# Two transformer blocks in one kernel: weight transfers in program order, and places for weights apart from places for working tiles

## The chip, the cores and the metric

The kernel runs on 1 core of one Trainium2 chip. The time is that of one execution on the device, in microseconds (us), and the number for a kernel is the median of its runs.

## The reference

The input is one sequence of 256 tokens of 1024 numbers. A first block of two layers and a second block of one follow one another:

```python
for l in range(2):                                  # first block
    h = h + hybrid_mixer(rmsnorm(h, norm_mix[l]), ...)       # dilated + window attention, gated
    h = h + expert_choice_ffn(rmsnorm(h, norm_ffn[l]), ...)  # 16 experts, 32 tokens each
x = rmsnorm(h, norm_final) + sincos                 # second block
s_f, s_b = context_states(hc @ w_in[:, 512:2048], lbs)       # from 256 context tokens
x = x + gt1 * token_mixer(modulate(rms_norm(x), sh1, sc1) @ w_in, ..., s_f, s_b)  # hgrn2 + hyena
x = x + gt2 * hier_moe(modulate(rms_norm(x), sh2, sc2), ...) # 4 groups x 8 experts, top 2
y = rms_norm(x, final_norm_g)
```

An expert of the first block computes silu(a) * u with a, u = its 32 tokens times 1024 x 1024 matrices, and multiplies by a third. The second block's experts are 1024 x 512. The modulation (sh, sc, gt) is a product of a 1024 vector with ada_w. All weights are 32-bit floats; the chip reads 745.74 MB of HBM in an execution.

## The kernel before

Weights stream through SBUF in chunks of 1 MB, [128 partitions x 2048 numbers], each fetched by `K.chunk(src)` (L51): it takes a tile named w with the tag W and issues one transfer on SyncE's queue (SP). The pool gives the tag W PLACES = 21 places of 8 KB per partition. The large working tiles (those named in WHOLE: x, hTa, hTb, V, G, hn, ob and so on) take their places out of the same 21. Small tags (P, PT, wh, wl, oa) have two to four places of 2 KB. The Tile scheduler decides in which order the instructions of an engine stand, SP's transfers among them; a transfer is issued when the place it writes is free, and all later ones on SP's queue stand behind it.

The stages, by the profile's time:
- Mixer 0 and mixer 1 (57 to 300, 637 to 1014): the projections w_in, w_a, w_b, w_o in blocks. Each chunk is split on ScalarE and VectorE into wh (L95) and wl (L96), and TensorE multiplies three times (L115 to L117). While it does so, the 24 chunks of ada are multiplied by the conditioning (L588) and attention goes on.
- Experts of layers 0 and 1 (310 to 637, 1022 to 1489): 128 chunks of w_eg (gate and up; eight a expert, L765) and 64 of w_ed (down, L816), used unsplit. In layer 0, chunks wk of the next layer's projection are computed among w_ed. In layer 1, preparation of the second block (long filter, context states) is woven into the experts. 19 chunks of w_eg are asked for ahead of the loop (PLACES - 2).
- Token mixer (1516 to 1800): chunks w2z, w2q, w2v, w2h, w2g, w2ga, w2gb, w2a, w2b, w2o, split as above. Ahead of it, the residual h is normed (hn, L178), transposed by TensorE (L187) and modulated; `gb` (a 256 KB tile of the tag P, L592) holds the bias of the modulation.
- Experts of the second block (1817 to 2291): per four experts 16 chunks of w2eg (L1427) and 8 of w2ed (L1468). 17 are asked for ahead of it. The last chunk of w2ed does not take a place of W: four quarters of it take three places of wh and one of wl (`quarters`, L62).

The stretches between these are the routers and norms. Small loads (masks, biases, constants; L45, L614, L1010) stand on the same queue.

Of the kernel before, what the change touches and what calls it, by code (L numbers as in the profile page):

```python
# [9 lines left out]
F = mybir.dt.float32  # L10
FR = mybir.dt.float32r
# [21 lines left out]
class Core:  # L33
    def __init__(self, ctx, tc, A):
# [19 lines left out]
    def next_chunk(self, src):  # L54
        return self.pre.pop(0) if self.pre else self.chunk(src)

    def quarters(self, src, tags):

        ts = []
        for i, tag in enumerate(tags):  # L60
            t = self.sb.tile([128, 512], F, name="w4", tag=tag, bufs=SMALL[tag])
            self.nc.sync.dma_start(out=t, in_=src[:, i * 512:(i + 1) * 512])  # L62
            ts.append(t)
        return Quarters(ts)
# [224 lines left out]
PLACES = 21  # L289
# [25 lines left out]
def mixer(K, h, l, ada, first=None, ahead=None):  # L315
# [225 lines left out]
    for c in range(2):  # L541
# [3 lines left out]

        K.row_blocks([K.chunk(A["w_o"][l, 2 * c + i]) for i in range(2)], mT, add, ("sc", "mm")[c])
# [33 lines left out]
def ada_gate(K, g):  # L580
# [11 lines left out]
    nc.sync.dma_start(out=gb, in_=K.A["gtb"][g])  # L592
# [18 lines left out]
def first_loads(K):  # L611
    nc, A = K.nc, K.A
    K.negd = K.t([128, 1280], "negd", tag="cA")
    nc.sync.dma_start(out=K.negd, in_=A["negd"])  # L614
# [3 lines left out]
    nc.sync.dma_start(out=K.wr, in_=A["wr"])  # L618
# [55 lines left out]
def experts(K, h, l, mix, ada, prep, ahead=None):  # L674
# [75 lines left out]
    ws = [K.chunk(A["w_eg"][l, i // KD, i % KD]) for i in range(PLACES - 2)]  # L750
# [105 lines left out]
def context(K):  # L856
# [16 lines left out]
    nc.sync.dma_start(out=cx, in_=A["ctx"])  # L873
# [55 lines left out]
def long_filter(K):  # L929
# [4 lines left out]
    for t, n in ((w1, "hw1"), (w2, "hw2"), (zT, "hz")):  # L934
        nc.sync.dma_start(out=t, in_=A[n])
# [36 lines left out]
    nc.sync.dma_start(out=dft, in_=A["dftf"])  # L972
# [11 lines left out]
def token_mixer(K, h):  # L984
# [279 lines left out]
    K.wr = K.t([128, KD, 64], "wr2", tag="wr")  # L1264
    nc.sync.dma_start(out=K.wr, in_=A["wr2"])
    for c in range(2):
# [6 lines left out]
        K.row_blocks([K.chunk(A["w2o"][c, i]) for i in range(2)], mT, add, ("sc", "mm")[c])  # L1273
# [3 lines left out]
def moe(K, h, mix):  # L1277
# [416 lines left out]
```

## Time and profile before

| | us |
|---|---|
| median of 3 runs | 2315.32 (2307.85 to 2316.28) |
| profiled execution | 2309.24 |
| its span in the profile | 2307.5 |
| TensorE busy | 1843.7 (80%) |
| VectorE, ScalarE, GpSimd busy | 780.5, 584.2, 215.9 |

The DMA engines moved 748.84 MB, a mean of 325 GB/s. A share of 80% for TensorE is a mean over stages: it is over 90% in the mixers and about 70% in the experts.

### The profile page before, as it was taken

To read this page: it belongs to the slowest core of one execution; us is meant where nothing else is said; L and a number is where in the kernel's file an instruction comes from. 1 tells how busy PE (TensorE), PEld (TensorE's weight loads), DVE (VectorE), ACT (ScalarE), POOL (GpSimd) and SP (SyncE) were. 2 spreads that over 40 slices of the span, in tenths; PEclk is the share of its full clock that TensorE was granted. 3 is DMA by queue.
4 is the path that set the end of the run, shared out by engine and by line. 5 is a ranking of instruction groups with operands and counts; after the bars stand their busy time and mean duration, and the time that the engine had idled before them with its cause. 6 is when DMAs were issued, how large, how long until landed. Compare 5 with 4: busy or idle time off the path is not lost. (4 is left out here: it accounts for less than half of the span.)

```text
span 2307.5 us, 30259 instructions
## 1 busy us (share of the span) xinstructions
PE 1843.7 (80%) x12172; PEld 1041.9 (45%) x12172; DVE 780.5 (34%) x1823; ACT 584.2 (25%) x1181; POOL 215.9 (9%) x179
## 2 busy tenths in 40 slices
PE   8999896666699989988678667589999877676665
PEld 7877741110277776742234123268787412121211
DVE  4765530000045687632112011237546311111112
ACT  4555410000032354530126000055235200000000
POOL 2101300000011111300000000034033000000000
PEclk9999997777799988998889788889999999999988
DMA  8335679999999920879999999882114899999996
GB/s 348 111 128 219 246 315 420 420 420 420 419 419 418 409 105 1 349 300 402 420 419 419 419 420 419 331 330 94 72 73 169 329 420 419 420 419 420 419 420 262
DMA packets 108442, 748.84 MB, mean 325 GB/s; under 512 B 14119, under 2 KB 14536, under 8 KB 18696
## 3 DMA queue, kind: packets, MB, share of 16 engines
q1 hardware_dynamic: 107752, 745.79, 79.4%
q8 instruction: 98, 1.61, 0.3%
q10 hardware_dynamic: 544, 1.05, 0.1%
q14 instruction: 48, 0.39, 0.0%
HBM read 745.74 MB, written 1.05 MB: 324 GB/s over the span
## 5 line engine op out<-in xcount | busy, mean ns | idle before, releaser
L765 PE MATMUL mm<-w,xT 128*32 128x512 f32 x2048 | 317.6, 722 | 106.4 <-DMA w<-in_w_eg 106.1
L95 ACT ACTIVATE wh<-w 128x512 fp32r<-128x512 f32 x384 | 234.8, 628 | 306.7 <-PE mm L116 214.8
L115 PE MATMUL mm<-hTa,wh 128*128 128x256 f32 x960 | 283.6, 297 | 14.6 <-ACT wh L95 10.7
L117 PE MATMUL mm<-hTa,wl 128*128 128x256 f32 x960 | 277.0, 293 | 7.8 <-DVE wl L96 6.8
L116 PE MATMUL mm<-hTb,wh 128*128 128x256 f32 x960 | 275.1, 288 | 1.6 <-DVE hTb L107 1.6
L96 DVE TENSOR_TENSOR wl<-w,wh 128x512 fp32r<-128x512 f32 x286 | 212.6, 757 | 113.0 <-ACT wh L95 109.9
L1427 PE MATMUL mm<-w,xT 128*32 128x512 f32 x1024 | 179.2, 625 | 71.7 <-DMA w<-in_w2eg 71.3
L816 PE MATMUL acc<-w,hid 128*32 128x256 f32 x2048 | 176.5, 445 | 63.1 <-DMA w<-in_w_ed 63.1
L96 POOL TENSOR_TENSOR wl<-w,wh 128x512 fp32r<-128x512 f32 x98 | 127.9, 1305 | 921.4 <-ACT wh L95 827.8
L115 PEld LDWEIGHTS mm<-hTa,wh 128*128 128x128 f32 x960 | 185.2, 193 | 36.6 <-ACT wh L95 17.9
L765 PEld LDWEIGHTS mm<-w,xT 128*32 128x32 f32 x2048 | 51.2, 118 | 312.7 <-DMA w<-in_w_eg 250.6
L117 PEld LDWEIGHTS mm<-hTa,wl 128*128 128x128 f32 x960 | 183.4, 193 | 19.4 <-DVE wl L96 9.6
L116 PEld LDWEIGHTS mm<-hTb,wh 128*128 128x128 f32 x960 | 185.5, 193 | 5.3 <-issue 2.8
L816 PEld LDWEIGHTS acc<-w,hid 128*32 128x32 f32 x2048 | 79.9, 127 | 144.7 <-DMA w<-in_w_ed 83.0
L1468 PE MATMUL acc<-w,work 128*32 128x512 f32 x512 | 104.9, 677 | 35.5 <-DMA w<-in_w2ed 32.7
L1427 PEld LDWEIGHTS mm<-w,xT 128*32 128x32 f32 x1024 | 34.7, 111 | 194.2 <-DMA w<-in_w2eg 144.7
L172 POOL TENSOR_TENSOR rs<-rs,mhalf 128x2 f32<-128x2 f32 x9 | 6.7, 748 | 1013.3 <-DVE rs L171 1013.3
L781 DVE TENSOR_TENSOR hid<-tp,sg 128x256 f32<-128x256 f32 x32 | 13.6, 425 | 218.1 <-ACT sg L780 218.1
L107 DVE SCALAR_TENSOR_TENSOR yd<-acc,gw,yd 128x256 fp32r<-128x256 f32 x32 | 15.4, 483 | 173.4 <-ACT yd L106 173.4
L85 DVE COPY gs<-mm 128x512 f32<-128x512 f32 x16 | 11.1, 692 | 176.2 <-PE mm L765 176.2
L1468 PEld LDWEIGHTS acc<-w,work 128*32 128x32 f32 x512 | 21.1, 121 | 107.5 <-issue 58.8
L106 ACT ACTIVATE yd<-acc,gw 128x256 fp32r<-128x256 f32 x32 | 15.1, 472 | 209.1 <-PE acc L816 209.1
(468 smaller groups left out, 2517.9 us busy)
## 6 DMA issues: line engine op xcount, KB each, us to landing
w<-in_w_eg SPq DMA_DIRECT2D x256, 1024.0 KB, 19.9
w<-in_w_ed SPq DMA_DIRECT2D x128, 1024.0 KB, 19.9
w<-in_w2eg SPq DMA_DIRECT2D x128, 1024.0 KB, 19.9
w<-in_w2ed SPq DMA_DIRECT2D x63, 1024.0 KB, 19.9
w<-in_ada SPq DMA_DIRECT2D x24, 1024.0 KB, 8.0
w<-in_w_in SPq DMA_DIRECT2D x22, 1024.0 KB, 12.8
w<-in_wk SPq DMA_DIRECT2D x20, 1024.0 KB, 19.3
w<-in_w_b SPq DMA_DIRECT2D x8, 1024.0 KB, 7.3
```

What stands on the lines that cost most here:

```text
L95: self.hi = nc.scalar.activation(hi, src, AF.Copy)
L96: (nc.gpsimd if n in self.idle or n % 4 == 3 else nc.vector).tensor_tensor(lo, src, hi.bitcast(F), OP.subtract)
L106: nc.scalar.activation(hi, src, AF.Identity, scale=scale)
L107: nc.vector.scalar_tensor_tensor(lo, src, scale, hi.bitcast(F), op0=OP.mult, op1=OP.subtract)
L115: mm(out, lhsT=l[0], rhs=r[0], start=start, stop=False)
L116: mm(out, lhsT=l[0], rhs=r[1], start=False, stop=False)
L117: mm(out, lhsT=l[1], rhs=r[0], start=False, stop=stop)
L765: nc.tensor.matmul(gu[32 * j:32 * j + 32, :], lhsT=xT[:, k, (e % 8) * CAP:(e % 8 + 1) * CAP], rhs=w[:, j * 512:(j + 1) * 512], start=(k == ...
L781: nc.vector.tensor_mul(hid[-1][:, e % 8], pv[:, :, 64:128], sg)
L816: nc.tensor.matmul(dn[32 * x:32 * x + 32, :T], lhsT=hid[e // 8][:, e % 8, f, hh * 32:hh * 32 + 32], rhs=ws[x][:, fb * T:(fb + 1) * T], sta ...
L1427: nc.tensor.matmul(gu[o:o + 32, :], lhsT=xT[:, k, y:y + CAP2], rhs=ws[x][:, (2 * kk + j) * 512:(2 * kk + j + 1) * 512], start=(k == 0), st ...
L1468: nc.tensor.matmul(dn[32 * x:32 * x + 32, :], lhsT=hid[x][:, c, :], rhs=wd[x][:, c * 512:(c + 1) * 512], start=(c == 0), stop=(c == 3), ti ...
```

## The change

Every transfer on SP's queue now goes through `fetch`, which orders it behind the one fetched before it in the program. The tag W has nine places for weights alone, the new tag T twelve for the working tiles of WHOLE. Where the program knows some of the twelve to be free, a chunk may take one of them: `use(places)` sets a ring of W and T from which the following chunks take their tags in turn. ROOM is the ring for the 19 chunks ahead of an expert loop of the first block, ROOM2 for the 16 of the second, FEW (nine W, two T) for later ones.

```diff
+    def use(self, places):
+        self.ring = cycle(places)
+
+    def fetch(self, out, src):
+        with self.tc.issue_after(self.sent.ins) if self.sent else nullcontext():
+            self.sent = self.nc.sync.dma_start(out=out, in_=self.A[src] if isinstance(src, str) else src)
+
-    def chunk(self, src):
-        t = self.sb.tile([128, PW], F, name="w", tag="W", bufs=PLACES)
-        self.nc.sync.dma_start(out=t[:, :src.shape[1]], in_=src)
+    def chunk(self, src, parts=1):
+        tag = next(self.ring)
+        t = self.sb.tile([128, PW], F, name="w", tag=tag, bufs=PLACES[tag])
+        n = src.shape[1] // parts
+        for i in range(parts):
+            self.fetch(t[:, i * n:(i + 1) * n], src[:, i * n:(i + 1) * n])
         return t
...
         if tag in WHOLE:
-            tag, bufs = "W", PLACES
+            tag, bufs = "T", PLACES["T"]
...
-PLACES = 21
+ROOM2 = "TWWTTTTWWTTTWWWW"
+ROOM, FEW = "TWWWWTTTTTTWWTTTWWW", "WWWWTWWWWWT"
+PLACES = {"W": 9, "T": 12}
...
-    ob = (K.t([128, 8, T], "ob0", tag="hn", dt=FR), K.t([128, 8, T], "ob1", tag="ob", dt=FR))
+    ob = []
...
+        K.use("W" if c else "T")
         K.row_blocks([K.chunk(A["w_o"][l, 2 * c + i]) for i in range(2)], mT, add, ("sc", "mm")[c])
...
-    ws = [K.chunk(A["w_eg"][l, i // KD, i % KD]) for i in range(PLACES - 2)]
+    K.use(ROOM)
+    ws = [K.chunk(A["w_eg"][l, i // KD, i % KD]) for i in range(len(ROOM))]
+    K.use("WT" if ahead else FEW)
...
+            if q == 1 and y == 0:
+                K.use(FEW)
             ws = [K.chunk(A["w_ed"][l, q, 4 * y + x]) for x in range(4)]
...
-    K.wr = K.t([128, KD, 64], "wr2", tag="wr")
-    nc.sync.dma_start(out=K.wr, in_=A["wr2"])
...
+        K.use("W" if c else "T")
+        ws = [K.chunk(A["w2o"][c, i]) for i in range(2)]
+        K.use("W")
+        if c == 0:
+            K.wr = K.t([128, KD, 64], "wr2", tag="wr")
+            K.fetch(K.wr, "wr2")
...
+    K.use(ROOM2)
     K.pre = [K.chunk(A["w2eg"][2 * i + x, c]) for i in range(2) for c in range(4) for x in range(2)]
-    K.pre.append(K.chunk(A["w2ed"][0, 0]))
-    K.gf = K.t([128, D], "gf2", tag="cA")
-    nc.sync.dma_start(out=K.gf, in_=A["gfin2"])
+    K.use("WWTWT")
...
-        wd = [K.next_chunk(A["w2ed"][e + x, hf]) for x in range(3 if end else 4)]
-        if end:
-            wd.append(K.quarters(A["w2ed"][e + 3, hf], ("wh", "wh", "wh", "wl")))
+        wd = [K.next_chunk(A["w2ed"][e + x, hf], 4 if end and x == 3 else 1) for x in range(4)]
```

Here `ahead` is true in layer 0. The other lines of the diff replace `nc.sync.dma_start` by `K.fetch` and move the load of gf2 into the routing.

SP's queue at the start, before (each row is a transfer, tile<-tensor; the rows left out are small loads of the same kind):

```order
L45 DMA qsc<-in_qsc 128x14
L614 DMA negd<-in_negd 128x1280
L45 DMA sink<-in_sink 128x32
L45 DMA bgate<-in_bgate 128x32
L45 DMA gffn<-in_gffn 128x16
...
L45 DMA fr<-in_fr 64x4
L45 DMA lbp<-in_lbp 128x16
L51 DMA w<-in_w_in 128x2048 x15
```

SP's queue at the start, after:

```order
L56 DMA qsc<-in_qsc 128x14
L56 DMA w<-in_w_in 128x2048 x5
L56 DMA negd<-in_negd 128x1280
L56 DMA sink<-in_sink 128x32
L56 DMA bgate<-in_bgate 128x32
L56 DMA gffn<-in_gffn 128x16
```

Five chunks of w_in moved ahead of the small loads, and fr and lbp away from them.

TensorE from the last w_ed (L802 adds its result) to the token mixer, before; L187 are the transposes of hn, L588 the products with the four ada chunks, L115 to L117 those with w2z:

```order
L802 MATMUL sc<-yd,Ge_9763 128x256 x4
L187 MATMUL tp<-ident,hn 128x128 x16
L588 MATMUL acc<-w,cs_591 32x512 x16
L115 MATMUL mm<-hTa,wh 128x256
L116 MATMUL mm<-hTb,wh 128x256
L117 MATMUL mm<-hTa,wl 128x256
```

TensorE at the same place, after (L597 is the former L588, L191 the former L187, L119 the former L115):

```order
L813 MATMUL sc<-yd,Ge_9763 128x256 x4
L597 MATMUL acc<-w,cs_591 32x512 x16
L191 MATMUL tp<-ident,hn 128x128 x12
L119 MATMUL mm<-hTa,wh 128x256
L120 MATMUL mm<-hTb,wh 128x256
L121 MATMUL mm<-hTa,wl 128x256
L119 MATMUL mm<-hTa,wh 128x256 x2
```

The sixteen products with ada moved from behind the transposes to ahead of them, and the last four transposes behind the first products with w2z.

SP's queue ahead of the second block's experts, before; L62 are the four quarters of the last w2ed chunk:

```order
L1265 DMA wr_13165<-in_wr 128x512
L51 DMA w<-in_w2b 128x2048
L51 DMA w<-in_w2o 128x2048 x4
L51 DMA w<-in_ada 128x2048 x4
L62 DMA w_15338<-in_w2ed 128x512
L62 DMA w_15332<-in_w2ed 128x512
L62 DMA w_15334<-in_w2ed 128x512
L62 DMA w_15336<-in_w2ed 128x512
L592 DMA gb<-in_gtb 128x512
L51 DMA w<-in_w2eg 128x2048 x16
L51 DMA w<-in_w2ed 128x2048
```

SP's queue at the same place, after:

```order
L56 DMA w<-in_w2o 128x2048 x2
L56 DMA wr_13169<-in_wr 128x512
L56 DMA w<-in_w2o 128x2048 x2
L56 DMA w<-in_ada 128x2048 x4
L56 DMA gb<-in_gtb 128x512
L56 DMA w<-in_w2eg 128x2048 x16
L56 DMA gf_13662<-in_gfin 128x1024
```

The quarters are gone from there (the last four rows of w2ed, 128x512, stand at the end of the stream now), and wr moved behind two chunks of w2o.

## Rows read from the trace of the kernel before

**Rows 1.** Windows by stretch: each engine's busy us (count), clock granted, DMA share, GB/s.
```profile
310.00:637.00 327.00, 222.37 (x1400) 55.33 (x1398) 21.00 (x41) 18.36 (x38) 0.00 (x0) 0.79 1.01 417
...
637.00:1014.00 377.00, 351.94 (x2625) 268.24 (x2626) 244.35 (x581) 158.78 (x351) 66.99 (x53) 0.93 0.71 286
...
1022.00:1489.00 467.00, 346.79 (x2469) 140.61 (x2468) 67.15 (x150) 80.46 (x126) 0.70 (x1) 0.87 1.01 414
...
1782.00:1797.00 15.00, 14.07 (x56) 10.12 (x57) 5.85 (x9) 6.78 (x14) 3.04 (x3) 0.89 0.00 1
...
1797.00:2287.00 490.00, 346.51 (x1876) 103.11 (x1875) 81.91 (x195) 39.10 (x74) 1.97 (x2) 0.94 1.00 413
```

**Rows 2.** Waits of TensorE, 1015 to 1490: total us, times, longest.
```profile
PE acc L816 <- DMA w<-in_w_ed: 48.0, 36, 1.9
PE mm L765 <- DMA w<-in_w_eg: 30.1, 27, 1.4
```

**Rows 3.** Timeline of SP's queue, start: start us, length, line, transfer.
```profile
5.72 0.43 SPq L614 DMA_DIRECT2D negd<-in_negd  x1
...
15.22 5.59 SPq L51 DMA_DIRECT2D w<-in_w_in  x9
```

**Rows 4.** Timeline of TensorE, start.
```profile
21.25 0.38 PE L115 MATMUL mm<-hTa,wh 128*128 128x256 f32 x1 [3.01 <-ACT wh L95]
```

**Rows 5.** Timeline of SP's queue, first experts of layer 0.
```profile
309.31 2.38 SPq L51 DMA_DIRECT2D w<-in_w_eg  x2
```

**Rows 6.** Timeline of TensorE, first experts of layers 0 and 1.
```profile
316.41 1.06 PE L765 MATMUL mm<-w,xT 128*32 128x512 f32 x8
...
1017.90 1.07 PE L765 MATMUL mm<-w,xT 128*32 128x512 f32 x8
...
1042.71 4.50 PE L765 MATMUL mm<-w,xT 128*32 128x512 f32 x40
```

**Rows 7.** Windows at the heads of both layers' experts.
```profile
309.00:322.00 13.00, 13.00 (x84) 5.27 (x80) 1.83 (x4) 2.23 (x3) 0.00 (x0) 1.00 0.87 324
...
1020.00:1034.00 14.00, 13.28 (x85) 5.62 (x84) 1.45 (x3) 2.69 (x4) 0.00 (x0) 1.00 0.84 328
1034.00:1045.00 11.00, 10.59 (x72) 5.42 (x68) 2.27 (x5) 2.30 (x6) 0.00 (x0) 1.00 1.00 416
1045.00:1050.00 5.00, 4.18 (x44) 1.31 (x38) 1.11 (x2) 0.38 (x1) 0.00 (x0) 1.00 1.01 421
```

**Rows 8.** Window in layer 1's mixer.
```profile
862.00:890.00 28.00, 26.36 (x92) 15.37 (x93) 18.78 (x88) 14.18 (x50) 0.00 (x0) 0.57 0.00 1
```

**Rows 9.** Timeline of TensorE, from layer 1 to the token mixer.
```profile
1501.94 1.97 PE L187 MATMUL tp<-ident,hn 128*128 128x128 f32 x8 [11.09 <-DVE hn L178]
...
1515.57 0.39 PE L115 MATMUL mm<-hTa,wh 128*128 128x256 f32 x1 [2.10 <-ACT wh L95]
```

**Rows 10.** Timeline of SP's queue, same place.
```profile
1498.20 2.26 SPq L51 DMA_DIRECT2D w<-in_ada  x4
1500.51 2.00 SPq L51 DMA_DIRECT2D w<-in_w2z  x4
```

**Rows 11.** Timeline of SP's queue, ahead of the second block's experts.
```profile
1796.10 3.32 SPq L62 DMA_DIRECT2D w<-in_w2ed  x4
...
1799.95 26.25 SPq L51 DMA_DIRECT2D w<-in_w2eg  x16
```

**Rows 12.** Timeline of GpSimd, same place.
```profile
1781.20 1.26 POOL L1271 TENSOR_TENSOR h<-h,P 128x512 f32<-128x512 f32 x1 [2.50 <-DVE P L1269]
```

**Rows 13.** Timeline of TensorE: first matmuls of w2eg, last group of w2ed.
```profile
1817.10 1.51 PE L1427 MATMUL mm<-w,xT 128*32 128x512 f32 x8
...
2287.39 3.64 PE L1468 MATMUL acc<-w,work 128*32 128x512 f32 x32
```

**Rows 14.** Transfers issued in 1760 to 1840: count, KB each, median us to landing.
```profile
w<-in_w2ed SPq DMA_DIRECT2D x4, 256.0 KB, 3.8
```

**Rows 15.** Page, part 6, transfers of the whole run.
```profile
w<-in_w_eg SPq DMA_DIRECT2D x256, 1024.0 KB, 19.9
```

More of the change, by code (lines that the diff above doesn't have):

```diff
@@ L1 @@
 from contextlib import ExitStack, nullcontext
-from itertools import islice
+from itertools import cycle, islice
 import numpy as np
@@ L40, in __init__, with next_chunk @@
         self.after = nullcontext
-        self.idle, self.pre = (), []
+        self.idle, self.pre, self.sent = (), [], None
+        self.use("W")
     def load(self, name, shape, dt=F):
         t = self.const.tile(shape, dt, name=name)
-        self.nc.sync.dma_start(out=t, in_=self.A[name])
+        self.fetch(t, name)
         return t
-    def chunk(self, src):
-        t = self.sb.tile([128, PW], F, name="w", tag="W", bufs=PLACES)
-        self.nc.sync.dma_start(out=t[:, :src.shape[1]], in_=src)
-        return t
[L54 to L64, printed above, removed]
+    def use(self, places):
[9 more added lines that the diff above has]
+            self.fetch(t[:, i * n:(i + 1) * n], src[:, i * n:(i + 1) * n])
+        return t
+    def next_chunk(self, src, parts=1):
+        return self.pre.pop(0) if self.pre else self.chunk(src, parts)
     def bank(self, tag):
@@ L491, in window @@
                                      rhs=PTs[half][:, kt * 256:(kt + 1) * 256], start=(kt == 0), stop=(kt == 1))
+            if not ob:
+                ob.extend(K.t([128, 8, T], f"ob{i}", tag="ob", dt=FR) for i in range(2))
             K.split_to(ob[0][:, pair, :], ob[1][:, pair, :], po)
@@ L591, in ada_gate @@
     gb = K.t([128, 512], "gb", NP, tag="P")
-    nc.sync.dma_start(out=gb, in_=K.A["gtb"][g])
+    K.fetch(gb, K.A["gtb"][g])
     K.ms = K.t([128, 512], "ms", tag="wr")
@@ L613, in first_loads @@
     K.negd = K.t([128, 1280], "negd", tag="cA")
-    nc.sync.dma_start(out=K.negd, in_=A["negd"])
+    K.fetch(K.negd, "negd")
     K.sink, K.bgate = K.load("sink", [128, L, 16]), K.load("bgate", [128, L, 16])
@@ L617, in first_loads @@
     K.wr = K.t([128, L, KD, 32], "wr")
-    nc.sync.dma_start(out=K.wr, in_=A["wr"])
+    K.fetch(K.wr, "wr")
     K.iota, K.fold = K.load("iota", [128, CAP2 + 1]), K.load("fold", [128, 96])
@@ L872, in context @@
     cx = K.t([128, 2, D], "cx", tag="hn")
-    nc.sync.dma_start(out=cx, in_=A["ctx"])
+    K.fetch(cx, "ctx")
     rs = K.rstd(cx)
@@ L934, in long_filter @@
     for t, n in ((w1, "hw1"), (w2, "hw2"), (zT, "hz")):
-        nc.sync.dma_start(out=t, in_=A[n])
+        K.fetch(t, n)
     def sine(p, nb):
@@ L971, in long_filter @@
     dft = K.t([128, 2, 2, T], "dft", tag="qb")
-    nc.sync.dma_start(out=dft, in_=A["dftf"])
+    K.fetch(dft, "dftf")
     K.KS = K.t([128, 2, 2, 512], "KS", tag="ob")
@@ L987, in token_mixer @@
     sc = K.t([128, 2, D], "sincos", tag="V")
-    nc.sync.dma_start(out=sc, in_=A["sincos"])
+    K.fetch(sc, "sincos")
     gf = K.t([128, D], "gf", tag="qc")
-    nc.sync.dma_start(out=gf, in_=A["gfin1"])
+    K.fetch(gf, "gfin1")
     hg = K.t([128, 2, D], "hg", tag="hgw")
@@ L1271, in add @@
             (nc.vector if tt else nc.gpsimd).tensor_add(hs, hs, t1)
-        K.row_blocks([K.chunk(A["w2o"][c, i]) for i in range(2)], mT, add, ("sc", "mm")[c])
+        K.use("W" if c else "T")
+        ws = [K.chunk(A["w2o"][c, i]) for i in range(2)]
+        K.use("W")
+        if c == 0:
+            K.wr = K.t([128, KD, 64], "wr2", tag="wr")
+            K.fetch(K.wr, "wr2")
+        K.row_blocks(ws, mT, add, ("sc", "mm")[c])
         yield
@@ L1384, in moe @@
         with tc.For_i(0, T // CAP2 - 1, 1):
+            K.sent = None
             nc.vector.tensor_scalar(slot, slot, -float(CAP2), None, op0=OP.add)
@@ L1505, in body @@
                 t = K.t([128, 512], "w4", NP, tag="PT")
-                nc.sync.dma_start(out=t, in_=A["w_in"][0, :, i * 512:(i + 1) * 512])
+                K.fetch(t, A["w_in"][0, :, i * 512:(i + 1) * 512])
                 first.append(t)
```

20 lines of the change are left out of this document (12 added, 8 removed).

## The prediction

> **What bounds the kernel now.** I read the times of the stretches first. In three of them the DMA engines carry 413 to 417 GB/s at a share of 1.00 or 1.01, while TensorE is busy 222 of 327, 347 of 467 and 347 of 490 us: layer 0's experts (310 to 637), layer 1's (1022 to 1489) and the second block's (1797 to 2287). They are bound by the stream of weights [rows 1]. Between them the reader sees the reverse: in 637 to 1014 TensorE is busy 352 of 377 us and DMA has share 0.71 [rows 1]. The chain of waits in layer 1's experts agrees: 48.0 us on w_ed and 30.1 on w_eg, in waits of at most 1.9 us [rows 2]. So a microsecond in which the DMA engines stand still inside a DMA stretch, or start it late, is a microsecond of the end; inside a mixer it costs nothing as long as the next weight lies ready. A stretch ends when its last byte is there, so every term below is one of two kinds: DMA's idle time at the head of a DMA stretch, or TensorE's idle time in one that TensorE bounds.
>
> The profiled execution took 2309.24 us (span 2307.5), 6.1 us under the median of the three runs, 2315.32. I sum on the profiled time and put the difference on the median. 1 MB chunks are 1.049 MB and at 420 GB/s move in 2.5 us.
>
> **The change, part by part.**
>
> Start. Before, the queue issues sixteen small loads from 5.72 on and the first nine w_in chunks only from 15.22 [rows 3]; TensorE then stands 3.01 us at 21.25 for the split of a chunk that came late [rows 4]. The order listing puts five w_in chunks ahead of negd, so w_in 1 is issued at about 6, 9 us earlier, and lands long before 18. What the small loads feed is late instead, by five chunks, 12.5 us at most; the cover is the first w_in chunks, which TensorE multiplies meanwhile. The idle 3.0 goes, and with it part of a stretch at half clock that follows it (an estimate of 1 us): **−4**; bounds 0 (some small load is needed at once) and −5.
>
> Layer 0's first experts. Before, w_eg 19 goes out at 309.31 [rows 5]. In the new ring, w_eg 19 takes the W place of chunk 1, w_eg 20 asks for the T place of chunk 6, whose last matmul runs at 316.41 to 317.47 [rows 6]. All later chunks stand behind it in the queue. Up to 322 before carried 4.21 MB (324 GB/s for 13 us [rows 7]); after carries chunk 19 (1.05 MB) and what flows from 317.5 plus the 1.4 us that before shows between issue and flow (13 us less 0.87 of 13, and 0.3 for the issue at 309.3 rather than 309.0): 3.1 us, 1.3 MB. The lack of 1.86 MB is 4.4 us: **+4.4**, bounds 2 and 5.7 (all of 317.5 − 309.3, less one chunk).
>
> Mixer 1. The mask loads and what stood behind them come free, but there TensorE waited for no weight. What changes is the order on TensorE: some 145 fill matmuls stand earlier and attention later. The rows cannot price that: 28 us ran at a granted 0.57 of the clock with 26.4 us busy [rows 8]. Were all of it at 1.00 it would save up to 12 us; if as much again fell to half, it would cost as much. I take **0**, bounds −12 and +12.
>
> Layer 1's first experts. This is the largest loss. The ring FEW gives w_eg 147 to 150 the W places of chunks 1 to 4, free at 1019.0 to 1025.1 (one more each 2.06 us, the first behind the row at 1017.90), 151 the T place of chunk 6 (five such steps on, 1029.2), and then w_eg 152 a W place again. The next W place is that of chunk 11, the first of the forty matmul rows from 1042.71, free at 1043.8; 153 that of chunk 12; 154 that of chunk 16, later still [rows 6]. So five chunks flow, then nothing from about 1034 to 1045, and the stream is whole only from there. Up to 1050 before carried 14 × 328 + 11 × 416 + 5 × 421 = 11.3 MB [rows 7]; after has 5.2 MB and 5 us at 420, 7.3 MB. The lack of 3.9 MB is 9.4 us. TensorE could make it up only if it were the bound later, but in layer 1's w_ed, the second part of the stretch, it still waits 48.0 us for weights [rows 2]: **+9.4**, bounds 5 (the ring's releases come earlier, since in that stretch TensorE no longer waits) and 12 (the ring asks late a second time).
>
> From layer 1 to the token mixer. TensorE starts on the transposes at 1501.94, after 11.09 us on hn; the 32 matmul records of ada stand behind them, and the first of w2z at 1515.57 after 2.10 more, ended by the split of a w2z chunk [rows 9]. The queue shows why: the four ada wait behind gtb until 1498.20, and w2z goes out at 1500.51 [rows 10]. After, ada stands ahead of gtb, behind the last w_ed, so that ada's matmuls fall into the idle 11 us (the order rows show them ahead of the transposes), and w2z goes out at about 1498.2 on a queue that is empty by 1500. It lands at about 1503 to 1505; transposes, casts and split end at about 1509: **−6**, bounds −3 (split behind ScalarE's eight ht) and −8.
>
> Token mixer itself: weights lie ready on both sides; **0 ± 3**.
>
> Second block's experts. This is the largest gain. The four quarters of the last w2ed chunk wait for places of wh and wl and go out only at 1796.10 and after, and gtb and w2eg 0 (1799.95) stand behind them [rows 11]; DMA share was 0.00 in 1782 to 1797 [rows 1]. After, the quarters are gone, and ahead of w2eg stand ada and gtb. gtb's place is free once GpSimd's h has run, 1781.20 to 1782.46 [rows 12]. So the stream can start at about 1783 rather than 1796.1. It must then not stall: sixteen w2eg last 16.8 MB, 40 us, to 1823. I take it that each finds its ROOM2 place free in that time, as the sixteen before went out within 26.25 us [rows 11]; and TensorE starts to free places at 1817.10 + 1.5 [rows 13]. The stretch has the same bytes: **−13.1**, bounds −2 (below) and −14.
>
> Tail. Before, the last 32 matmul records (3.64 us from 2287.39) begin only when all four chunks are there [rows 13]. After, the last chunk comes as four parts in the order in which they are used, and each matmul group waits for its part. Three quarters of the 3.64 can run while parts land: **−2**, bounds −2.7 and 0. Against it speaks the row of the quarters: a 256 KB transfer took 3.8 us from issue to landing [rows 14], though its bytes need 0.6. If that is a price that each part pays behind the one before, four parts need 15.2 us where one chunk needs 2.5 (rival D); if it is a latency that the others hide, nothing. I take the second, since the stream runs at 420 GB/s, a chunk each 2.5 us, although each takes 19.9 us from issue to landing [rows 15]: eight are in flight at once.
>
> The Trainium skill, page DMA: Bandwidth & Descriptors, section Anatomy of one DMA, speaks for the first: it gives every transfer a fixed 2.0 us, most of it the receipt of the last byte, beside its bytes. An estimate by it for four parts in a row is 10.4 us, the tail +6 and the sum −3.3; the row's 3.8 is above its 2.6 for one part, so the row doesn't contradict it, and no run here shows four parts behind one another.
>
> Sum: −4 + 4.4 + 0 + 9.4 − 6 + 0 − 13.1 − 2 = −11.3. On 2309.2 that is 2298; on the median of 2315.3, 2304. Faster or slower by 0.5%, 11.6 us, is about what a measurement of this kernel can tell from no change, so the sum lies on that line. The bounds of the unknown terms lean a little to the fast side (mixer 1 at half clock has more to win than to lose, since 42 us already run slow), so I put the likeliest at 2302.
>
> **Rivals.**
>
> A, the early start is not had. If gtb's place is not free when h is (four P places, and the next user of one may be later) the queue is blocked as before: −2 in place of −13.1, sum 0, 2315. Against it: the row of h; for it: the queue is strictly in order, and any one late place holds all.
>
> B, larger gain. Mixer 1 keeps the full clock, −12, or layer 1's releases come early enough that its stream hardly stops. Each is worth 9 to 12: sum −21 to −23, 2293. For it: the fills now stand where TensorE paused before; against it: VectorE is busy 18.8 of the same 28 us [rows 8] and sets much of that pace.
>
> C, slower. The ring with two T places in eleven looks only eleven chunks ahead (nine W places), where before had 21 places for everything, and at full rate some eight of them are in flight. A pause of TensorE in layer 1 longer than three chunks, 7.5 us, then empties the queue again. The waits on weights there are 1.9 us at most [rows 2], but the preparation of the second block is woven into the experts in pieces, and each piece holds back a release. Three further gaps like the first would cost 28 us: sum +17, 2332. It turns slower from about 23 us more of DMA idle time than counted.
>
> D, the parts of the last chunk go one behind the other: +12.7 in place of −2, sum +3.4, 2319.
>
> **How the numbers follow.** Likeliest (sum −4 to −20): 0.52; A 0.10; B 0.20; C 0.13; D 0.05. The likeliest alone has 2295 to 2311, and slightly over half of it lies past 11.6. Faster: 0.31 from the likeliest and 0.20 of B, with 0.01 of A, 0.52. Slower: C's 0.12 and 0.03 of mixer 1 at half clock, 0.15. Same: the rest, 0.33. The range takes in B whole and C's near half: 2281 to 2320.
>
> **What would show it.** In the trace after: no wait of TensorE at 18 to 21; DMA share 0 from 1034 to 1045 and w_eg 152 issued after chunk 11's last matmul; ada's matmuls ahead of the transposes and the first w2z matmul 6 us nearer to the last expert's; w2eg 0 issued some 35 us before TensorE's first w2eg matmul rather than 17; the last group's matmuls in four steps. Wrong would make it: DMA share under 1.00 inside 1050 to 1480 or after the w2eg start, a mixer 1 that is more than 6 us longer or shorter, or a late place ahead of w2eg.

## The result, and the profile after

The changed kernel takes 2251.97 us (median of 4 runs, 2250.04 to 2254.18), the kernel before 2313.63 us beside it: a ratio of 0.9737, 95% interval 0.9715 to 0.9759. It is 61 us faster, over five times the 11.3 us of the forecast's sum, and lies below the range. Medians and ranges here leave out two executions of the experiments (one of b1_quarters_last, one of e11_small_first) that ran 7 to 22% longer at a lower granted clock. The profiled execution's span is 2248.3 us against 2307.5. The page after begins:

```profile
span 2248.3 us, 30174 instructions
...
PE 1835.5 (82%) x12172; PEld 1023.2 (46%) x12172; DVE 785.7 (35%) x1823; ACT 589.4 (26%) x1183; POOL 221.0 (10%) x179
```

TensorE's busy time has hardly changed (1843.7 before): it fell by 26 us in the mixers and rose by 17 in the expert stretches, where TensorE is not the bound. What went, in sum, is time in which it stood still.

To see where, I cut both traces at the same pieces of TensorE's work: the first w_eg matmul of layer 0, the first and last of w_ed, and so on. Each stage runs from one mark to the next, in us of the profiled execution:

| stage | before | after | difference | forecast |
|---|---|---|---|---|
| start and mixer 0 | 303.3 | 290.0 | −13.3 | −4 |
| experts, layer 0 | 494.7 | 501.3 | +6.6 | +4.4 |
| mixer 1 and router | 217.8 | 202.1 | −15.7 | 0 |
| experts, layer 1 | 473.3 | 479.6 | +6.3 | +9.4 |
| to the first w2z matmul | 26.4 | 16.5 | −9.9 | −6 |
| token mixer | 283.2 | 268.1 | −15.1 | 0 |
| router | 18.3 | 19.6 | +1.3 | – |
| second block's experts, with the tail | 473.9 | 454.8 | −19.1 | −15.1 |

The differences sum to −58.9. By these marks layer 0's experts last, in the kernel before, to 798.0 and not to 637: w_ed is multiplied in 590.9 to 798.0, with the DMA engines at 417 GB/s.

```profile
590.90:798.00 207.10, 187.74 (x1830) 138.45 (x1829) 94.19 (x144) 57.37 (x103) 22.57 (x17) 0.95 1.01 417
```

So the stretch 637 to 1014, which the forecast read as bound by TensorE, begins with 161 us of w_ed; no term of its sum rests on that. The expert stretches after, as windows (w_eg and w_ed of layer 0, then of layer 1, then the second block; columns as in [rows 1]):

```profile
290.00:579.60 289.60, 200.98 (x1162) 44.22 (x1162) 17.98 (x45) 15.47 (x33) 0.00 (x0) 0.79 0.97 402
579.60:791.30 211.70, 193.25 (x1830) 138.69 (x1829) 91.51 (x144) 58.40 (x104) 22.33 (x17) 0.95 1.01 418
993.40:1312.20 318.80, 256.80 (x1421) 92.06 (x1422) 49.76 (x124) 75.77 (x113) 0.69 (x1) 0.84 0.96 396
1312.20:1473.00 160.80, 109.24 (x1085) 51.48 (x1084) 19.36 (x34) 7.84 (x18) 0.00 (x0) 0.84 1.01 420
1777.20:2232.00 454.80, 333.13 (x1829) 93.98 (x1828) 69.22 (x140) 32.22 (x60) 0.00 (x0) 0.94 1.00 417
```

The reader sees the DMA bound unchanged, 417 to 420 GB/s, except over the two w_eg stretches: 402 and 396 GB/s at a share of 0.97 and 0.96, for 407 and 406 in the same stretches before.

**The forecast dips.** In layer 0 the row that answers to 309 to 322 in [rows 7] has 142 GB/s, for 324:

```profile
295.70:308.70 13.00, 13.00 (x80) 5.43 (x76) 1.85 (x5) 2.23 (x3) 0.00 (x0) 1.00 0.37 142
```

In layer 1's first experts the windows of the changed kernel show the hole that the ring was to make:

```profile
993.00:1010.00 17.00, 16.87 (x102) 6.83 (x104) 1.94 (x4) 2.82 (x6) 0.00 (x0) 1.00 0.71 271
1010.00:1020.00 10.00, 10.00 (x60) 5.15 (x52) 1.78 (x4) 2.98 (x6) 0.00 (x0) 1.00 0.16 65
1020.00:1032.00 12.00, 11.19 (x102) 3.33 (x100) 1.60 (x3) 0.38 (x1) 0.00 (x0) 1.00 0.83 316
```

65 GB/s in 1010 to 1020, answering to the row of 1034 to 1045 in [rows 7], which had 416. The stage became 6.3 us longer, for 9.4 forecast.

**The step to the token mixer** (TensorE's timeline after):

```profile
1477.11 1.90 PE L597 MATMUL acc<-w,cs 128*32 128x512 f32 x8 [2.40 <-DMA w<-in_ada]
...
1486.33 1.61 PE L191 MATMUL tp<-ident,hn 128*128 128x128 f32 x8
...
1489.47 0.39 PE L119 MATMUL mm<-hTa,wh 128*128 128x256 f32 x1
```

The products with ada (L597) run from 1477.11, ahead of the transposes, in the time in which TensorE waited for hn before [rows 9], and the first w2z matmul comes 3.1 us behind the first transpose rather than 13.6.

**The second block's experts.** Before, the queue stood 47.2 us for the places of the four quarters, and a few us more:

```profile
SPq L62 <- DVE wl L96: 47.2, 1, 47.2
```

Timeline of SP's queue after, and the two waits ahead of gtb:

```profile
1745.64 0.33 SPq L56 DMA_DIRECT2D gb<-in_gtb  x1
...
1746.07 3.83 SPq L56 DMA_DIRECT2D w<-in_w2eg  x8
```

```profile
SPq L56 <- ACT mTa L107: 19.6, 1, 19.6
SPq L56 <- POOL h L1283: 18.8, 1, 18.8
```

w2eg goes out at 1746.07, 31.1 us ahead of its first matmul (1777.2); before it was 17.2 us [rows 11, 13]. gtb still holds the queue, for 38.4 us: 19.6 until ScalarE's mTa and 18.8 more until GpSimd's h.

**The mixers**, which the forecast put at zero. Windows of before over start and mixer 0, mixer 1, and the step with the token mixer:

```profile
0.00:303.30 303.30, 280.99 (x1833) 230.66 (x1833) 183.08 (x507) 150.73 (x333) 53.49 (x48) 0.97 0.57 212
798.00:1015.80 217.80, 195.46 (x1083) 144.31 (x1082) 155.51 (x447) 105.32 (x256) 44.42 (x36) 0.87 0.48 188
1489.20:1798.80 309.60, 276.56 (x1864) 236.69 (x1864) 171.15 (x319) 133.35 (x251) 92.06 (x74) 0.94 0.36 140
```

After:

```profile
0.00:290.00 290.00, 276.78 (x1830) 228.34 (x1830) 182.86 (x500) 150.42 (x332) 53.73 (x48) 0.98 0.59 222
791.30:993.40 202.10, 184.02 (x1084) 138.13 (x1084) 156.14 (x448) 106.91 (x256) 46.63 (x36) 0.92 0.50 193
1473.00:1757.50 284.50, 266.32 (x1865) 228.11 (x1864) 177.61 (x319) 133.40 (x251) 94.90 (x74) 0.99 0.43 167
```

The length less the busy time gives TensorE's idle time: 22.3, 22.3 and 33.0 us before, 13.2, 18.1 and 18.2 after. The length times what the mean granted clock lacks of 1.00 gives about what the half clock cost: 9, 28 and 19 us before, 6, 16 and 3 after. Idle time fell by 28 us and clock loss by about 31, against 54 us that these stretches became shorter (the two overlap where TensorE is idle at half clock). The matmuls are as many (1833 against 1830 records, 1083 against 1084, 1864 against 1865).

### The profile page after: what moved, and what is told of

It is laid out like the page before. It is cut to its first block, busy times and chain, and to the rows that moved or that the text cites. A ratio compares the mean times of both kernels' runs of the same rounds, so it can differ in the third digit from the quotient of the medians.

```text
span 2248.3 us, 30174 instructions
## 1 busy us (share of the span) xinstructions
PE 1835.5 (82%) x12172; PEld 1023.2 (46%) x12172; DVE 785.7 (35%) x1823; ACT 589.4 (26%) x1183; POOL 221.0 (10%) x179
## 4 chain that ended last, share of the span: by engine, by line
PE 42%; DMA 29%; issue 22%; DVE 5%; ACT 2%; POOL 0%; POOLq 0%; ACTq 0%; DVEq 0%; SPq 0%
DMA w<-in_w_eg 17%; DMA w<-in_w_ed 8%; PE mm L119 7%; PE mm L120 7%; PE mm L121 7%; PE acc L829 4%; PE mm L776 3%; PE sc L855 2%; DVE wl L100 1%; PE acc L496 1%; PE sc L481 1%; DMA w<-in_w2z 1%; PE acc L915 1%; PE acc L1194 1%; DMA cx<-in_ctx 1%
## 5 line engine op out<-in xcount | busy, mean ns | idle before, releaser
L776 PE MATMUL mm<-w,xT 128*32 128x512 f32 x2048 | 332.1, 749 | 110.9 <-DMA w<-in_w_eg 110.2
L99 ACT ACTIVATE wh<-w 128x512 fp32r<-128x512 f32 x384 | 239.5, 630 | 306.9 <-PE mm L120 234.7
L119 PE MATMUL mm<-hTa,wh 128*128 128x256 f32 x960 | 281.6, 295 | 4.6 <-ACT z L1040 1.4
L121 PE MATMUL mm<-hTa,wl 128*128 128x256 f32 x960 | 275.3, 290 | 3.5 <-DVE wl L100 3.3
L100 DVE TENSOR_TENSOR wl<-w,wh 128x512 fp32r<-128x512 f32 x286 | 220.1, 775 | 104.1 <-ACT wh L99 101.5
L1451 PE MATMUL mm<-w,xT 128*32 128x512 f32 x1024 | 184.0, 651 | 63.2 <-DMA w<-in_w2eg 62.7
L829 PE MATMUL acc<-w,hid 128*32 128x256 f32 x2048 | 182.3, 448 | 62.1 <-DMA w<-in_w_ed 62.1
L100 POOL TENSOR_TENSOR wl<-w,wh 128x512 fp32r<-128x512 f32 x98 | 129.6, 1323 | 925.3 <-ACT wh L99 819.3
L119 PEld LDWEIGHTS mm<-hTa,wh 128*128 128x128 f32 x960 | 181.9, 190 | 29.0 <-issue 14.7
L121 PEld LDWEIGHTS mm<-hTa,wl 128*128 128x128 f32 x960 | 181.2, 190 | 12.7 <-issue 5.7
L1490 PE MATMUL acc<-w,work 128*32 128x512 f32 x512 | 99.7, 672 | 27.4 <-DMA w<-in_w2ed 27.3
L792 DVE TENSOR_TENSOR hid<-tp,sg 128x256 f32<-128x256 f32 x32 | 13.6, 425 | 214.9 <-ACT sg L791 214.9
L110 ACT ACTIVATE yd<-acc,gw 128x256 fp32r<-128x256 f32 x32 | 15.2, 474 | 217.5 <-PE acc L829 217.5
L791 ACT ACTIVATE sg<-tp 128x256 f32<-128x256 f32 x32 | 12.3, 383 | 218.8 <-PE tp L788 218.8
## 6 DMA issues: line engine op xcount, KB each, us to landing
w<-in_w_ed SPq DMA_DIRECT2D x128, 1024.0 KB, 18.8
```

Source lines behind the costliest of these rows:

```text
L99: self.hi = nc.scalar.activation(hi, src, AF.Copy)
L100: (nc.gpsimd if n in self.idle or n % 4 == 3 else nc.vector).tensor_tensor(lo, src, hi.bitcast(F), OP.subtract)
L119: mm(out, lhsT=l[0], rhs=r[0], start=start, stop=False)
L121: mm(out, lhsT=l[1], rhs=r[0], start=False, stop=stop)
L776: nc.tensor.matmul(gu[32 * j:32 * j + 32, :], lhsT=xT[:, k, (e % 8) * CAP:(e % 8 + 1) * CAP], rhs=w[:, j * 512:(j + 1) * 512], start=(k == ...
L829: nc.tensor.matmul(dn[32 * x:32 * x + 32, :T], lhsT=hid[e // 8][:, e % 8, f, hh * 32:hh * 32 + 32], rhs=ws[x][:, fb * T:(fb + 1) * T], sta ...
```

## The experiments

Theory P: the mixers became shorter because the working tiles have places of their own, which changes the order of the instructions on TensorE; the order of the transfers gave only the second block's experts and the start. Rival W: it is the order of the transfers, by which weights lie ready earlier. A second question, Q, is which late place holds the queue ahead of the second block's experts.

Every kernel was timed beside the kernel before. Lengths of the same stages, us, of each profiled execution:

| kernel | median us | mixer 0 | exp. 0 | mixer 1 | exp. 1 | step | token mixer | exp. 2 |
|---|---|---|---|---|---|---|---|---|
| before | 2313.6 | 303.3 | 494.7 | 217.8 | 473.3 | 26.4 | 283.2 | 473.9 |
| after | 2252.0 | 290.0 | 501.3 | 202.1 | 479.6 | 16.5 | 268.1 | 454.8 |
| e1_order_one_kind | 2284.3 | 304.8 | 493.9 | 221.0 | 474.3 | 23.7 | 283.0 | 454.2 |
| e2_split_free_order | 2314.2 | 291.6 | 524.0 | 212.4 | 483.1 | 17.4 | 268.5 | 483.9 |
| b1_quarters_last | 2296.0 | 305.6 | 494.7 | 220.5 | 476.4 | 26.1 | 284.6 | 453.5 |
| e4_ring_wt | 2250.6 | 289.3 | 501.1 | 201.9 | 475.8 | 16.5 | 269.6 | 457.3 |
| e5_gtb_other_queue | 2244.6 | 288.7 | 500.5 | 202.6 | 481.7 | 16.8 | 268.3 | 448.9 |
| e6_no_lending | 2283.1 | 289.3 | 513.7 | 200.2 | 492.7 | 16.6 | 269.2 | 466.3 |
| e7_ring_gtb | 2239.5 | 289.0 | 501.2 | 202.1 | 475.9 | 17.6 | 267.0 | 449.3 |
| e11_small_first | 2257.6 | 290.7 | 500.1 | 200.0 | 479.8 | 15.9 | 271.1 | 453.9 |
| e12_tail_whole | 2251.4 | 289.5 | 501.2 | 201.9 | 479.5 | 16.4 | 268.2 | 456.5 |
| e13_wt_all | 2245.3 | 291.0 | 503.9 | 201.2 | 477.5 | 16.8 | 269.4 | 448.5 |
| e14_w_only_ed0 | 2243.0 | 289.0 | 501.2 | 205.2 | 475.7 | 17.6 | 268.6 | 448.0 |

Lengths that an edit can hardly reach differ by some 2 to 3 us from execution to execution: mixer 0 takes 303.3 us before and 305.6 in b1. The edits are against the changed kernel except where another is named.

**The transfers' order without the separate places.**

```diff
-        tag = next(self.ring)
+        tag = "W"
...
-            tag, bufs = "T", PLACES["T"]
+            tag, bufs = "W", PLACES["W"]
...
-PLACES = {"W": 9, "T": 12}
+PLACES = {"W": 21}
```

> All transfers in program order and no quarters, as in the changed kernel, but one kind of 21 places for weights and working tiles. TensorE's order is that of before but for 36 of 9712 matmuls. Theory P (the mixers gained because the separate places change TensorE's order there; the transfers' order gave only the start, the step to the token mixer and the second block's experts): about 2285 us, mixers as long as before (mixer 1 218 us, token mixer with its last projection 282 us). Rival W (the mixers gained because weights lie ready earlier): about 2255 us, mixers as short as after (202 and 267 us).

2284.25 us (2280.6 to 2291.73), ratio to before 0.9863 (0.9842 to 0.9883): the total of theory P, though in part by luck. Its windows over the three mixer stretches:

```profile
0.00:304.80 304.80, 284.51 (x1830) 234.37 (x1830) 181.26 (x501) 150.56 (x332) 53.46 (x48) 0.96 0.56 211
798.70:1019.70 221.00, 198.97 (x1084) 146.53 (x1084) 155.77 (x447) 105.13 (x256) 44.37 (x36) 0.86 0.48 183
1494.00:1800.70 306.70, 274.56 (x1864) 235.51 (x1864) 174.64 (x319) 133.21 (x251) 91.82 (x74) 0.95 0.41 159
```

Idle 20.3, 22.0 and 32.1 us, clock 0.96, 0.86 and 0.95: the mixers of before. So neither the order of the transfers, nor weights that lie ready earlier, nor the moved loads and the later ob tiles (all in this kernel) made the mixers faster. Its profiled execution (span 2289.9 us) is 17.6 us shorter than that of before, and the second block's experts alone make −19.7. Of the two other gains that theory P gave to the order, the start is not there (+1.5) and the step is small (−2.7). The profiled execution is the longest of the four, over 7 us above their median; where the others won these 7 no trace shows.

**The separate places without the transfers' order.**

```diff
-        with self.tc.issue_after(self.sent.ins) if self.sent else nullcontext():
+        with nullcontext():
```

> Nine places for weights, twelve for working tiles, rings and all as in the changed kernel, but the order of the transfers left to the scheduler. Theory P: the mixers are as short as after (mixer 1 about 202 us), in all 2260 to 2285 us. Rival W: the mixers are as long as before (218 us), 2295 us or more.

2314.15 us, ratio 1.0003 (0.9982 to 1.0023): the total lies where rival W put it, though the stages speak for theory P: mixer 0, the step and the token mixer are as short as after (291.6, 17.4 and 268.5), mixer 1 a third of the way (212.4). What was won is lost in the experts, by 29, 10 and 10 us. SP's queue around layer 0's w_ed, 580 to 820, shows how (total us, times, longest):

```profile
SPq L56 <- DVE wl L100: 102.3, 13, 18.4
SPq L56 <- PE acc L829: 71.0, 16, 11.2
```

and the window of that stretch:

```profile
582.30:815.60 233.30, 207.00 (x1818) 140.71 (x1817) 89.07 (x143) 58.28 (x102) 20.52 (x16) 0.91 0.93 376
```

Here a place is asked for that is free late (the longest waits 18.4 us on a split, 11.2 on a w_ed matmul), and what other places could take stands behind: 376 GB/s, where the changed kernel has 418. The order of the instructions differs from the changed kernel's too (by the traces in at least 885 of 12172 matmul records), so more than the transfers moved. The change needs both halves all the same: without the separate places it is worth 30 us (e1, with the quarters gone), without the order of the transfers nothing in the total. With both, the separate places win the mixers, and the program's order keeps the smaller store of weight places flowing.

**One part alone in the kernel before: the last chunk at the end.**

```diff
-        wd = [K.next_chunk(A["w2ed"][e + x, hf]) for x in range(3 if end else 4)]
-        if end:
-            wd.append(K.quarters(A["w2ed"][e + 3, hf], ("wh", "wh", "wh", "wl")))
+        wd = [K.next_chunk(A["w2ed"][e + x, hf]) if not (end and x == 3)
+              else K.chunk(A["w2ed"][e + x, hf], 4) for x in range(4)]
```

> The kernel before with one edit: the last chunk of w2ed takes a place of W in four parts at its turn, rather than quarters in wh and wl ahead of the experts. If the quarters at the queue's head cost the idle 13 us ahead of w2eg: 2298 us (15 us less than before). If gtb or another late place holds the queue there anyway: 2311 us or more.

2295.97 us (three runs, 2292.45 to 2298.24), ratio 0.9911 (0.9885 to 0.9937): 18 us less than the 2314.42 of the kernel before beside it, for 15 expected. SP's queue there:

```profile
1791.39 0.33 SPq L594 DMA_DIRECT2D gb<-in_gtb  x1
...
1791.77 26.34 SPq L53 DMA_DIRECT2D w<-in_w2eg  x16
```

w2eg goes out 35 us ahead of its first matmul (1826.8), and the stage takes 453.5 us, less than the changed kernel's 454.8. So the four quarters alone account for the gain of the second block's experts.

**The ring in layer 1.**

```diff
-    K.use("WT" if ahead else FEW)
+    K.use("WT")
```

> The changed kernel with one edit: the chunks of layer 1's w_eg after the first 19 take W and T in turn, as in layer 0, rather than nine W to two T. If the ring's late places cost layer 1's experts the 6 us that they became longer: 2246 us, and no DMA gap near the head of that stretch. If that length has another cause: 2252 us. A third outcome, slower than 2256 us, would mean that the working tiles of the second block's preparation miss the T places.

2250.57 us; the total can't tell it from the changed kernel. The windows can:

```profile
992.00:1010.00 18.00, 17.87 (x107) 7.09 (x107) 1.94 (x4) 3.55 (x6) 0.00 (x0) 1.00 0.33 120
1010.00:1020.00 10.00, 10.00 (x63) 5.20 (x65) 2.27 (x5) 2.17 (x5) 0.00 (x0) 1.00 1.02 427
1020.00:1032.00 12.00, 10.47 (x97) 3.10 (x90) 1.12 (x2) 0.98 (x2) 0.00 (x0) 1.00 1.01 420
```

No hole at 1010 to 1020: 427 GB/s. Layer 1's experts take 475.8 us, 3.8 less than after. The ring's late places cost these 3.8: the four kernels with this ring have 475.7 to 477.5 us there, the four with the other 479.5 to 481.7. The other 2.5 of the 6.3 are not this ring's, and little more than such lengths differ by; here too the stream starts slowly (120 GB/s in the first 18 us).

**gtb on another queue.**

```diff
-    K.fetch(gb, K.A["gtb"][g])
+    nc.gpsimd.dma_start(out=gb, in_=K.A["gtb"][g])
```

> The changed kernel with one edit: gtb goes out on GpSimd's queue, so that w2z and w2eg no longer stand behind its wait for a place. In the changed kernel that wait lasts 18.8 us on GpSimd's h ahead of w2eg, with DMA share 0.14 in 1716 to 1745. Theory Q (the head of the queue sets when the second block's experts end): w2eg starts 10 to 19 us earlier, 2235 to 2243 us. Rival: no place is free for w2eg before h, or TensorE becomes the bound: 2250 us or more.

2244.63 us, ratio 0.9705 (0.9679 to 0.9732): 7 us off, a little less than theory Q's 2235 to 2243 asks. The queue and two windows:

```profile
1715.87 54.27 SPq L56 DMA_DIRECT2D w<-in_w2eg  x16
```

```profile
1720.00:1740.00 20.00, 17.16 (x104) 14.39 (x104) 18.92 (x27) 9.65 (x20) 12.33 (x10) 1.00 0.78 305
1740.00:1760.00 20.00, 18.91 (x87) 14.00 (x85) 10.78 (x23) 7.05 (x15) 6.91 (x6) 1.00 0.68 263
```

The stream starts 30 us earlier, at 1715.87, but its sixteen chunks then need 54 us: behind the first ones the queue waits for places that matmuls over working tiles (L121), the last splits (L100) and ada's products (L597) give back:

```profile
SPq L56 <- PE mm L121: 28.0, 3, 11.2
SPq L56 <- DVE wl L100: 11.6, 3, 9.8
SPq L56 <- PE acc L597: 8.9, 3, 8.0
```

Taking one late place away uncovers the next.

**No lending.**

```diff
-        tag = next(self.ring)
+        tag = "W"
```

> The changed kernel with one edit: chunks take the nine W places alone and never one of the twelve T. Theory: nine places hold 22 us of the stream, so the steady stretches stay near 420 GB/s, but 10, 10 and 8 chunks fewer lie ready when the three expert stretches begin: up to 25 us lost in each where TensorE would work on from them, in all 2290 to 2325 us, with mixers as short as after. Rival (lending matters little, since eight transfers are in flight anyway): 2260 us or less.

2283.14 us, 7 us below the range expected: +12.4, +13.1 and +11.5 us in the three expert stretches, none in the mixers:

```profile
0.00:289.30 289.30, 276.17 (x1830) 227.58 (x1830) 182.84 (x501) 150.53 (x332) 53.71 (x48) 0.98 0.51 186
803.00:1003.20 200.20, 179.62 (x1085) 136.60 (x1083) 156.04 (x448) 106.55 (x256) 46.82 (x36) 0.94 0.41 150
1495.90:1781.70 285.80, 270.64 (x1865) 231.70 (x1864) 177.66 (x319) 133.63 (x251) 94.90 (x74) 0.97 0.43 164
```

Idle 13.1, 20.6 and 15.2 us. The lent places are worth 31 us in the median, all of it in the experts. And the mixers are as short with no lending at all, so it is the working tiles' own places that they gain from.

**Both helping edits together** (the edits of e4_ring_wt and e5_gtb_other_queue).

> The changed kernel with both edits that seem to help: W and T in turn in layer 1's experts (alone 2250.6 us), and gtb on GpSimd's queue. If the two are independent: the sum of both, 2233 to 2242 us.

2239.53 us (2238.67 to 2242.59), ratio to before 0.9684 (0.9661 to 0.9707), below the changed kernel's 0.9737 with no overlap. This is the lowest median of all versions, and faster than both kernels.

**The start.**

```diff
-            K.col_blocks(first if first and c == 0 else K.chunk(w), KD, x, emit_qd, 2 * c)
-        first_loads(K)
+            K.col_blocks(first if first and c == 0 else K.chunk(w), KD, x, emit_qd, 2 * c)
+            if c == 0:
+                first_loads(K)
```

> The changed kernel with one edit: the fifteen small loads stand ahead of w_in again, as before the change. Theory (w_in 1 to 5 first takes the 3 us pause at 21 away and that stays): first w_eg matmul 3 to 5 us later than the changed kernel's 290.0, in all 2255 us. Rival (the mixer swallows it): first w_eg matmul at 289 to 291, 2252 us. The time alone can't tell these apart, the profile's marks can.

The first w_eg matmul stands at 290.7, for 290.0: by this mark the rival is right, and the early w_in is worth nothing that lasts. The time does not say the same: 2257.63 us (three runs, 2249.87 to 2258.65), 6 us over the changed kernel, though the intervals of the ratio to before overlap (0.9732 to 0.979, and 0.9715 to 0.9759). The profiled execution is the shortest of the three, with the span of the changed kernel (2247.9 us), so no stage explains the 6 us, and they stay open.

**The tail.**

```diff
-        wd = [K.next_chunk(A["w2ed"][e + x, hf], 4 if end and x == 3 else 1) for x in range(4)]
+        wd = [K.next_chunk(A["w2ed"][e + x, hf], 1) for x in range(4)]
```

> The changed kernel with one edit: the last chunk of w2ed comes as one transfer of 1 MB rather than four of 256 KB. Theory (the matmuls of the last group run while parts land): the end comes 1 to 2 us later after the last byte, 2253 us. Rival D of the prediction, and the Trainium skill's fixed 2.0 us for each transfer (DMA: Bandwidth & Descriptors, Anatomy of one DMA): 6 to 13 us earlier, 2239 to 2246 us.

2251.36 us, no difference that can be measured; the stage is 1.7 us longer (456.5), which is within what it differs among kernels that have the parts (453.5 to 457.3). The last matmuls of the changed kernel, one run of 32 records while the parts land:

```profile
2227.33 4.66 PE L1490 MATMUL acc<-w,work 128*32 128x512 f32 x32
```

and with the whole chunk, six and then, after a pause, 26:

```profile
2226.36 1.38 PE L1490 MATMUL acc<-w,work 128*32 128x512 f32 x6
2229.14 3.62 PE L1490 MATMUL acc<-w,work 128*32 128x512 f32 x26 [1.41 <-SPq L1406]
```

Rival D is refuted: four transfers of 256 KB cost no more than one of 1 MB here. The Trainium skill (DMA: Bandwidth & Descriptors, section Anatomy of one DMA) gives a transfer a fixed 2.0 us and puts most of it down to the receipt of the last byte; its figure is for transfers issued from GpSimd, and these go out on SyncE's queue. Here the four parts together are not 6 us dearer than the whole, as the estimate from that figure had them, so it is not paid once for each part behind the other.

**Two tries at layer 0's w_ed**, which became 4.6 us longer (211.7 for 207.1 us). The first, beside the two edits of e7_ring_gtb:

```diff
             if q == 1 and y == 0:
-                K.use(FEW)
+                K.use("WWT" if ahead else FEW)
```

> The two edits that helped together (2239.5 us) and one more: in layer 0's w_ed, from its second quarter on, chunks take W, W, T in turn rather than nine W to two T. If the ring costs the 4.6 us by which layer 0's w_ed became longer: that stretch 207 us and 2235 us in all. If the longer stretch has another cause (TensorE's order among the next layer's projections): no change, 2239 us. If the working tiles of the next layer miss the places: slower, 2245 us or more.

2245.33 us (2244.12 to 2256.17), the third of the outcomes named: that stretch took 214.3 us, and by the trace's landings its last w_ed chunk was there 498.0 us after the first w_eg matmul, for 489.1 in the changed kernel. The second has `"W" if ahead` in that line:

> The two edits that helped together (2239.5 us) and one more: in layer 0's w_ed, from its second quarter on, chunks take W places alone. That stretch took 207 us with no lending, 212 with two T in eleven, 214 with one T in three. If lending there delays the next layer's working tiles: that stretch 207 to 208 us, in all 2235 us. If not: no change, 2239 us.

2243.01 us (2235.24 to 2254.26), that stretch 211.5: no change. So lending from the second quarter of w_ed on is not the cause of these 4.6 us. Lending before it is not excluded: with no lending at all (e6) the stretch takes 206.5.

## Why the prediction was wrong

The step that failed is the pricing of the mixers: "Mixer 1 ... I take **0**, bounds −12 and +12", "Token mixer itself: weights lie ready on both sides; **0 ± 3**", and mixer 0 not priced at all beyond its start. These three gave −13.3, −15.7 and −15.1 us for the −4 forecast: 40 of the 47.6 us that were missed. The reasoning was that a mixer, bound by TensorE, gains nothing from transfers as long as weights lie ready. e1_order_one_kind bears that out. But the change had a second half: the working tiles got places of their own, and with them the scheduler put the instructions in another order. For mixer 1 the forecast named the new order on TensorE and left it at 0 within 12 us either way, and the 15.7 lie past that; for mixer 0 and the token mixer it did not price the order at all. By the traces (operations and tiles in order of time) at least 915 of 12172 matmul records stand elsewhere after than before, 29 in e1. The other engines were reordered too: 142 of ScalarE's 1181 instructions (5 in e1) and 355 of VectorE's 1823 (27).

Shown: the separate places make mixer 0 and the token mixer short, with the program's order of transfers or without it (e2), with lending or without (e6); the order alone doesn't (e1). Mixer 1 is short with the separate places and the program's order (202.1, and 200.2 in e6), but only a third of the way there without that order (212.4 in e2). Shown by the windows: the gain is idle time and half clock, in about equal parts. Argued, not shown: that the new order of instructions does it, rather than a wait for a place at run time, and which engine's order counts. For the order speaks that in the mixers of before I find no wait of ScalarE, VectorE or GpSimd that ends when a weight chunk's place comes free. A run with before's order and the new places would settle it; the scheduler makes the order out of the places, and there is no such run.

How a pause can cost twice is seen in mixer 1 of before. TensorE's timeline, and three windows around it:

```profile
836.50 0.38 PE L115 MATMUL mm<-hTa,wh 128*128 128x256 f32 x1 [1.03 <-ACT wh L95]
...
839.98 1.94 PE L445 MATMUL tp<-ident,P 128*128 128x128 f32 x8 [2.45 <-DVE P L419]
...
860.27 0.63 PE L445 MATMUL tp<-ident,P 128*128 128x128 f32 x4 [2.07 <-DVE P L419]
...
863.60 0.58 PE L474 MATMUL sc<-kx,q 128*128 128x256 f32 x1 [1.52 <-ACT kx L365]
```

```profile
830.00:838.00 8.00, 6.48 (x54) 5.26 (x52) 7.81 (x31) 6.32 (x15) 0.38 (x1) 1.00 0.26 108
838.00:852.00 14.00, 12.03 (x48) 9.66 (x50) 11.18 (x34) 4.10 (x9) 0.88 (x1) 0.52 0.21 65
852.00:862.00 10.00, 7.18 (x66) 6.00 (x62) 8.54 (x21) 5.60 (x13) 1.27 (x1) 1.00 0.35 120
```

A pause of 1.03 us ends at 836.50 and one of 2.45 at 839.98, and from 838 to 852 the granted clock is 0.52, nearly all of it at the lower of its two levels, 1.2 GHz; the next pauses, to 863.6, stand beside the start of the 28 us at 0.57 of [rows 8]. I had that row, and called its sign unknown.

The other steps, one by one:
- Start, −4: wrong. The pause at 21 us is gone in e1_order_one_kind too (0.9 us left), but its first w_eg matmul comes at 304.8, no earlier than before. What is won in the first 20 us is swallowed by mixer 0, and the −13.3 of the changed kernel are mixer 0's.
- Layer 0's head, +4.4: right in mechanism and nearly in size. By the trace's landings, counted from the first w_eg matmul, the thirtieth chunk of w_eg landed at 42.8 us, for 38.5 before: 4.3 us late. The lag is still 3.1 us at the fifty-sixth chunk of w_ed (462.4 for 459.3). So the split of the stage's +6.6 into 2.0 in w_eg and 4.6 in w_ed does not say where it arose: most of it fits the head, and the rest stays open. That the lag sets the stage's end is not shown either: in e14 the last w_ed chunk landed 2.8 us later than in the changed kernel, and the stage was as long.
- Layer 1's head, +9.4: the hole is where the ledger of places put it, 17 us behind the first w_eg matmul, and nearly as costly: the sixtieth chunk of w_eg landed 8.7 us late (127.4 for 118.7). What the forecast left out is that the stream catches up: the last chunk of w_ed is 6.2 us late (475.9 for 469.7), w_ed flowing at 420 GB/s rather than 412, and the stage is 6.3 longer. Taking the hole away gives back 3.8 (e4).
- Step to the token mixer, −6: mechanism as forecast, −9.9. But not from the order of the transfers: e1 has it, keeps ada's products behind the transposes and takes 23.7 us. ada's products moved ahead with the separate places.
- Second block's experts, −13.1 and −2: right in kind, −19.1 measured, −20.4 with the last chunk's place alone changed (b1). The stream was issued 13.9 us earlier relative to its first matmul, as forecast; but its first chunk landed 17.4 us earlier (26.1 ahead of that matmul, for 8.7), and its last w2eg chunk 17.9 earlier. The tail's −2 fits the 1.7 of e12, which the spread of the stage does not let one tell from nothing; the last group's matmuls run as one row of 32, not in the four steps foretold. The two prices of rival D don't match: +12.7 takes nothing off for matmuls that run while parts land, +6 takes off 2.
- Rival A did not happen: gtb held the queue only until h, as the forecast of 1783 had counted. Of rival B, mixer 1's −12 came, and more. Rival C, further gaps by the short ring, did not: the stream of layer 1 loses nothing more behind the first hole.

## What to carry to other kernels

A change to a pool is a change to the order of every engine that the scheduler fills: compare the orders first and price each stage that moves, above all the ones that an engine bounds, before counting transfers. Where a stage bound by TensorE has a mean granted clock below 1.00 (0.87 in mixer 1 of before, about 28 us), look for the short pauses beside its slow stretches. And on a queue that issues in order, look for the one transfer whose place comes free last: here four quarters of one chunk cost 18 us, and the 256 KB behind them 7 more.

## What the runs showed of the hardware that I had not expected

The granted clock fell to its lower level around pauses as short as 1.03 and 2.45 us (ending at 836.50 and 839.98 in mixer 1 of before), with TensorE busy 6.48 us of 830 to 838. That the pauses brought it down is read from their place beside it; no run took them out alone. Four transfers of 256 KB at the end of a stream were as cheap as one of 1 MB, within 2 us (2251.97 and 2251.36 us in all).
